# Feed-forward up products taken on x times the norm weight, with the root of the norm applied behind them

## The chip, the core and the metric

The kernel runs on one core of a Trainium2 chip. The metric is the device time of one execution in microseconds (us), as the median of several runs. The kernel works in float32 kept as two halves: each operand is split into a rounded part ("h") and a rest ("l"), and each product is the sum of three passes of TensorE, h·h, h·l and l·h. TensorE (PE) multiplies, VectorE (DVE) makes the rests and the sums, ScalarE (ACT) makes the rounded parts and the activations, GpSimd (POOL) starts accumulating transfers, and SyncE (SP) starts the loads.

## What is computed

One macaron block: a feed-forward (FFN), a mixer, a second FFN and a last norm, on 512 tokens of width 1024; the hidden width of an FFN is 2816, or 22 tiles of 128 columns. Cut to what matters here:

```python
def rmsnorm(x, g):
    y = x * lax.rsqrt(jnp.mean(x * x, axis=-1, keepdims=True) + EPS)
    return y * g

def swiglu(x, w_gu, w_down):
    g, u = jnp.split(x @ w_gu, 2, axis=-1)
    return (jax.nn.silu(g) * u) @ w_down

x = x + 0.5 * swiglu(rmsnorm(x, g1), ffn1_w_gu, ffn1_w_down)
x = x + hybrid_mixer(rmsnorm(x, gm), w_in, ...)
x = x + 0.5 * swiglu(rmsnorm(x, g2), ffn2_w_gu, ffn2_w_down)
return rmsnorm(x, gf)
```

The root, 1/sqrt(mean(x²) + eps), is one number for each token. It can be put on x before the product, or on the product's rows after it.

## The kernel before

Activations lie transposed: `x[k]` is the k-th 128 of the 1024 columns, by 512 tokens. An FFN's up half makes 22 hidden tiles, each from a gate column block and an up column block of 128.

**Three kinds of products.** A *plain* tile multiplies weights (stationary) with x (moving, 512 tokens): 2 column blocks, 8 depths and 3 passes, 48 passes of 512 columns each. A *tall set* makes four tiles by seven products in place of eight, from sums of blocks of the weights and of the activations; it has 14 steps (7 products in two halves) of 12 passes of 512 columns, 168 passes, with the activations stationary and the weights moving. A *set* makes two tiles by the same seven products in 168 passes of 256 columns. The products are named m1, p2, q6, p5, q7, p3 and p4; m1, q6, q7 and p4 add up in one PSUM bank, and what is in it has to be copied out by ACT before the next of them is added. A tall set's result has tokens on the partitions, so it is turned by `turn`: 16 transposes of 128x128 on PE.

**Order before.** Each FFN takes the first four hidden tiles as plain tiles, on x times the norm weight (no root), and multiplies the results with the root, `row`, laid out along the tokens (`plain_pair`). FFN 1 then has four tall sets and a set, FFN 2 a tall set, a set and three tall sets. Those work on the fully normed x: `normed` writes x·g·row into eight free tiles of `hid` (L757), and `Operands.make` splits its blocks and block sums (L676, L677). The class `Norm` splits x·g as each x[k] comes (L499, L500) and adds the squares (L505, L508, L509); `rstd_rows` sums them with two products against ones (L529, L530), transposes, takes the root and spreads it.

**What sets the order.** A scheduler places the instructions of each engine; each engine runs its queue in that order, and within the sets the order of PE is written by hand. Weights come as tiles of 512 KB named `f` (ten buffers) on SP's queue (L358). `Weights.issue` casts each to `wh` on ACT (L393) and makes the rest `wl` on DVE (L394), two steps ahead of the product. The sums of weight blocks are made in place: by transfers that add `f` to `f`, started on POOL (L362), and by subtractions on DVE (L372 for a tall set, and L387 for a set's extra sum). The mixer between the FFNs starts with loads of two small arrays, `wgl` and `gup` (L1140, L1153), into its buffers `tp`; the products of `wgl` are L1165 and L1166. It ends with the output products of `w_o`, of which eight tiles x[0] to x[7] are finished one after the other on DVE (L1624).

Of the kernel before, what the change touches and what calls it, by code (L numbers as in the profile page):

```python
# [8 lines left out]
F32 = mybir.dt.float32  # L9
# [94 lines left out]
PLAIN1, PLAIN2 = 4, 4  # L104
# [27 lines left out]
TALL_ORDER = ("m1", "p2", "q6", "p5", "q7", "p3", "p4")  # L132
TALL = {}


def tall(name, mat, cols, base=0):
# [6 lines left out]
    STEPS.extend((n, p) for p in TALL_ORDER for n in firsts)  # L143

# [13 lines left out]
def up_plan(up, plain, slow):  # L158

    kinds = ["tall"] * ((KF - plain) // 4)  # L160
    kinds.insert(len(kinds) if slow else 1, "set")
    f = plain
    for kind in kinds:
        if kind == "tall":
            tall((up, f), up, (f * P, DFF + f * P))
# [8 lines left out]
UPS = {}  # L174


def ffn_plan(up, down, plain, slow):
# [38 lines left out]
ffn_plan("ffn1_w_gu", "ffn1_w_down", PLAIN1, True)  # L216
mixer_plan()
ffn_plan("ffn2_w_gu", "ffn2_w_down", PLAIN2, False)
# [8 lines left out]
def block_kernel(ctx: ExitStack, tc: tile.TileContext, xT, vecs, gf, gup, wgl, wts, out):  # L227
# [79 lines left out]
    class Weights:  # L307
# [15 lines left out]
        def phase(self, early, first=6):  # L323
# [4 lines left out]
            for i in range(lo, self.end):  # L328
                n, p = STEPS[i]
                if p == "m1" and n in TALL:  # L330
                    self.loads.setdefault(i - (4, 3)[TALL[n][1]], []).append(n)
                    self.firsts.setdefault(i - (1, 0)[TALL[n][1]], []).append(n)
# [31 lines left out]
        def issue(self):  # L364
            at = self.issued
            self.fetch(at)
            for n in self.loads.get(at, ()):
                self.raw[n] = [self.dma(n + i) for i in range(4)]
# [144 lines left out]

    def rstd_rows(accs, width):
# [47 lines left out]
    class Set:  # L562
# [8 lines left out]

        def run(self, p):
            b = {"m1": "b", "p2": "a", "q6": "b", "p5": "c", "q7": "b", "p4": "b", "p3": "c"}[p]
            if self.group.joint:
                return self.run_joint(p, b)
# [6 lines left out]
            for k in range(4):  # L582
                for e in range(2):
                    s = slice(k * HW + e * P, k * HW + (e + 1) * P)
                    t = slice(k * HW, (k + 1) * HW)
                    to = o[:, e * HW : (e + 1) * HW]
                    for j, (ww, aa) in enumerate(((h, bh), (h, bl), (l, bh))):
# [9 lines left out]
        def run_joint(self, p, b):  # L597
            fresh = b not in self.bank
            two_banks = b != "b"
            if fresh:  # L600
                self.bank[b] = MM2() if two_banks else MM()
            o = self.bank[b]
            parts = self.group.get(p)
            h, l = W.take()
            for k in range(4):
                a = parts[k // 2][:, (k % 2) * S : (k % 2 + 1) * S]
                for e in range(2):
                    s = slice(k * HW + e * P, k * HW + (e + 1) * P)
                    if two_banks:
                        nc.tensor.matmul(o[:, e], h[:, s], a, start=fresh and k == 0,  # L610
                                         stop=False, skip_group_check=True)
                        nc.tensor.matmul(o[:, e, HW:], l[:, s], a[:, :HW], start=False,
                                         stop=k == 3, skip_group_check=True)
                        continue
                    to = o[:, e * HW : (e + 1) * HW]
                    for j, (ww, aa) in enumerate(((h, a[:, :HW]), (h, a[:, HW:]),
                                                  (l, a[:, :HW]))):
                        nc.tensor.matmul(to, ww[:, s], aa, start=fresh and k == 0 and e == 0 and j == 0,
                                         stop=k == 3 and j == 2, skip_group_check=True)
            if p in self.keep:  # L620
                v = T()
                nc.scalar.copy(v, o)
                self.v[p] = v
            self.done(self, p)

    class Operands:
# [5 lines left out]
        def __init__(self, b, joint=False):  # L632
            self.b = b
            self.joint = joint
            self.parts = {}
            self.sums = set()
# [20 lines left out]
        def make(self, p):  # L657
            if p in self.parts:
                return
            i = self.ORDER.index(p)  # L660
            if i > 0:
                self.make(self.ORDER[i - 1])
            v = self.sum(p)
            if self.joint:
                t = [tile_of("op", [P, 1024], F32R) for _ in range(2)]
                for i in range(2):
                    a = t[i].rearrange("p (k b t) -> p k b t", b=2, t=HW)
                    vi = v[:, 2 * i : 2 * i + 2]
                    nc.scalar.copy(a[:, :, 0], vi)
                    nc.vector.tensor_tensor(out=a[:, :, 1], in0=vi,  # L670
                                            in1=a[:, :, 0].bitcast(F32), op=ALU.subtract)
                self.parts[p] = t
                return
# [61 lines left out]
    def ffn(up, down, norm, nxt, plain, at):  # L735
        xh, xl = norm.h, norm.l
        rows = []

        def finish(k):
            if k == at:  # L740
                rows.append(norm.finish())
# [35 lines left out]
        for f in range(2, plain):  # L777
            g = mm_single(up, KD, f * P, xh, xl)
            u = mm_single(up, KD, DFF + f * P, xh, xl)
            if f == 2:  # L780
                xo.make("p5")
# [916 lines left out]
```

## Time and profile before

| | |
|---|---|
| Median of 3 runs | 1174.08 us (1173.42 to 1174.63) |
| The profiled execution | 1173.56 us, of which its span is 1171.8 us |
| PE busy | 1161.5 us, 99% of the span |
| DVE busy | 899.6 us, 77% |
| ACT busy | 643.0 us, 55% |
| Up half of FFN 1, from the first product on x to the first down product | 5.7 to about 230 us |
| Mixer | about 343 to 829 us |
| Up half of FFN 2 | about 829 to 1064 us |

A row of the timeline reads: start, duration, engine, line, operation, output and inputs with the buffer numbers left out, shape, count; in square brackets how long the engine had been idle and what ended it. "PEclk" is the granted share of the TensorE clock.

### The profile page before, as it was taken

The numbers are of one execution on the slowest core, as the hardware profiler recorded it, in microseconds if no ns is written. First come the engines' busy times: TensorE is split into PE (matmuls) and PEld (weight loads), VectorE is DVE, ScalarE is ACT, GpSimd is POOL, SyncE is SP. The second block draws the span as 40 slices with busy tenths as digits, with TensorE's granted clock in tenths as the row PEclk, the third lists the DMA queues.
The fourth block names the chain that finished last, engine by engine and source line by source line (L and its number), as shares of the span: only waits on it lengthen the run. The fifth ranks groups of instructions, "written<-read, shape, count | busy, mean of one in ns | idle before, by whom it ended". The sixth has DMA issues, their size and how long they took to land.

```text
span 1171.8 us, 16449 instructions
## 1 busy us (share of the span) xinstructions
PE 1161.5 (99%) x6410; PEld 1012.3 (86%) x6410; DVE 899.6 (77%) x1081; ACT 643.0 (55%) x811; POOL 121.6 (10%) x161
## 2 busy tenths in 40 slices
PE   9999999999999999999999999999999999999997
PEld 8888888999988888789999998888888988888886
DVE  7985657879887976777797999556598566699965
ACT  6555555635452757474654577524356555575543
POOL 0101110011110110111010112000010111101100
PEclk9999999999999999999999999999999999999999
DMA  9667785647485485877566788811746777867711
GB/s 362 132 187 170 173 221 154 170 121 180 104 283 144 93 219 155 201 206 208 141 162 158 176 201 220 288 36 50 247 112 158 195 191 155 205 177 171 179 49 72
DMA packets 59006, 200.07 MB, mean 171 GB/s; under 512 B 6865, under 2 KB 6993, under 8 KB 58929
## 3 DMA queue, kind: packets, MB, share of 16 engines
q0 software_dynamic: 19424, 70.26, 31.7%
q1 hardware_dynamic: 36912, 124.27, 31.5%
q10 hardware_dynamic: 2592, 4.49, 1.0%
q8 instruction: 50, 0.82, 0.3%
q14 instruction: 28, 0.22, 0.1%
HBM read 124.55 MB, written 8.39 MB: 113 GB/s over the span
## 4 chain that ended last, share of the span: by engine, by line
PE 96%; DVE 2%; ACT 1%; issue 1%; DMA 0%; POOL 0%; DVEq 0%; ACTq 0%; POOLq 0%
PE mm L704 44%; PE mm L588 22%; PE mm L445 7%; PE mm L422 3%; PE mm L423 3%; PE mm L421 3%; PE mm L464 1%; PE mm L463 1%; PE mm L462 1%; PE aux L826 1%; PE mm L1020 1%; PE mm L1018 1%; PE mm L1019 1%; DVE wl L394 1%; PE aux L1320 1%
## 5 line engine op out<-in xcount | busy, mean ns | idle before, releaser
L393 ACT CAST wh<-f 128x1024 fp32r<-128x1024 f32 (+1 forms) x343 | 359.2, 1048 | 381.2 <-PE mm L704 120.3
L394 DVE TENSOR_TENSOR wl<-f,wh 128x1024 fp32r<-128x1024 f32 (+1 forms) x343 | 416.8, 1218 | 184.9 <-ACT wh L393 180.1
L704 PE MATMUL mm<-wh,op 128*128 128x512 f32 x1568 | 492.4, 391 | 0.0
L704 PEld LDWEIGHTS mm<-wh,op 128*128 128x128 f32 x1568 | 294.4, 188 | 60.4
L704 PE MATMUL mm<-wl,op 128*128 128x512 f32 x784 | 305.7, 390 | 0.7 <-DVE wl L394 0.7
L588 PE MATMUL mm<-op,wh 128*128 128x256 f32 x1568 | 284.6, 284 | 0.6 <-ACT tp L593 0.6
L588 PEld LDWEIGHTS mm<-op,wh 128*128 128x128 f32 x1568 | 245.0, 192 | 1.7 <-ACT tp L593 0.8
L588 PE MATMUL mm<-op,wl 128*128 128x256 f32 x784 | 222.2, 283 | 1.1 <-DVE wl L394 1.1
L362 POOL DMA_DIRECT2D f<-f x126 | 108.6, 863 | 919.4 <-DVE wl L394 336.4
L704 PEld LDWEIGHTS mm<-wl,op 128*128 128x128 f32 x784 | 147.3, 188 | 31.2 <-DVE wl L394 1.5
L588 PEld LDWEIGHTS mm<-op,wl 128*128 128x128 f32 x784 | 150.3, 192 | 1.6 <-DVE wl L394 1.5
L445 PE MATMUL mm<-op,wh 128*128 128x512 f32 x256 | 64.0, 391 | 0.0
L421 PE MATMUL mm<-op,wh 128*128 128x512 f32 x164 | 63.8, 389 | 0.0
L422 PE MATMUL mm<-op,wh 128*128 128x512 f32 x164 | 63.8, 389 | 0.0
L423 PE MATMUL mm<-op,wl 128*128 128x512 f32 x164 | 63.8, 389 | 0.0
L445 PEld LDWEIGHTS mm<-op,wh 128*128 128x128 f32 x256 | 48.0, 188 | 10.3 <-issue 0.2
L676 ACT CAST op<-hid 128x1024 fp32r<-128x1024 f32 x42 | 43.9, 1048 | 18.7 <-PE mm L704 12.7
L677 DVE TENSOR_TENSOR op<-hid,op 128x1024 fp32r<-128x1024 f32 x42 | 51.2, 1220 | 3.6 <-ACT op L676 3.4
L387 DVE TENSOR_TENSOR f<-f,f 128x1024 f32<-128x1024 f32 x28 | 34.2, 1221 | 5.6 <-DMA f<-f 4.6
L421 PEld LDWEIGHTS mm<-op,wh 128*128 128x128 f32 x164 | 30.8, 188 | 6.5
L422 PEld LDWEIGHTS mm<-op,wh 128*128 128x128 f32 x164 | 30.8, 188 | 6.4
L423 PEld LDWEIGHTS mm<-op,wl 128*128 128x128 f32 x164 | 30.8, 188 | 6.3
(283 smaller groups left out, 1146.0 us busy)
## 6 DMA issues: line engine op xcount, KB each, us to landing
f<-wts SPq DMA_DIRECT2D x219, 512.0 KB, 4.3
f<-f POOLq DMA_DIRECT2D x126, 512.0 KB, 5.0
X<-xT SPq DMA_DIRECT2D x8, 256.0 KB, 5.3
xs<-X POOLq DMA_DIRECT2D x8, 256.0 KB, 6.3
ga<-tp ACTq DMA_DIRECT2D x8, 256.0 KB, 4.9
gb<-tp ACTq DMA_DIRECT2D x8, 256.0 KB, 3.8
tp<-ga SPq DMA_DIRECT2D x8, 256.0 KB, 4.8
X<-xs POOLq DMA_DIRECT2D x8, 256.0 KB, 7.4
```

The lines of the kernel that those rows point to most:

```text
L362: nc.gpsimd.dma_start(out_, a, accum_op=ALU.add)
L387: nc.vector.tensor_tensor(out=a11, in0=a11, in1=a22, op=ALU.subtract)
L393: nc.scalar.copy(h[:, :w], raw[:, :w])
L394: nc.vector.tensor_tensor(out=l[:, :w], in0=raw[:, :w], in1=h[:, :w].bitcast(F32), op=ALU.subtract)
L421: nc.tensor.matmul(o, wh, ah, start=first, stop=False)
L422: nc.tensor.matmul(o, wh, al, start=False, stop=False)
L423: nc.tensor.matmul(o, wl, ah, start=False, stop=last)
L445: nc.tensor.matmul(o[c], w[:, s : s + P], a[k], start=k == 0 and j == 0, stop=k == kt - 1 and j == 2)
L588: nc.tensor.matmul(to, ww[:, s], aa[:, t], start=fresh and k == 0 and e == 0 and j == 0, stop=k == 3 and j == 2, skip_group_check=True)
L676: nc.scalar.copy(hv, v)
L677: nc.vector.tensor_tensor(out=lv, in0=v, in1=hv.bitcast(F32), op=ALU.subtract)
L704: nc.tensor.matmul(self.bank[b][e], aa[:, c], ww, start=fresh and i == 0 and n == 0, stop=k == 3 and n == 2, skip_group_check=True)
```

## The change

The new class `Gain` takes the place of `Norm` for the two FFNs. The up products are taken on x·g, and the root is applied to their results: as the scale of the Silu and in the multiplication behind it. In tall sets the tokens lie on the partitions, so the root is a column of 128 numbers per token block: `finish` sums the squares by four products of one column each (L569) and takes the root on 128x4 numbers; nothing is transposed or spread.

In FFN 1 the first two hidden tiles stay plain, but with activations stationary and the four weight blocks moving (`GU`), and their results are turned on PE (`turn_pair`, 8 transposes); the other 20 are five tall sets. In FFN 2 nothing is plain: a tall set, a set, and four tall sets, the set with activations stationary (`Turned`) and turned by `turn_pair`. For the tall sets x·g is written whole into the free tiles of `hid` by eight ACT instructions (L773). In FFN 1 `Gain` besides splits it as x comes, in blocks of 256 tokens, which serve as operands of the plain tiles and of the products m1, p2 and p3. The order of the products differs by set: the first tall set of FFN 1 takes p5 ahead of q6, the first and last of FFN 2 take p5 ahead of p2. The first down products of FFN 1 leave two of the eight banks for the end, so that the last tall set can be turned in between, and the buffers `tp` of the mixer move behind its others.

```diff
-PLAIN1, PLAIN2 = 4, 4
+FIRST1 = ("m1", "p2", "p5", "q6", "q7", "p3", "p4")
+FIRST2 = ("m1", "p5", "p2", "q6", "q7", "p3", "p4")
...
-def up_plan(up, plain, slow):
+def up_plan(up, first):
-    kinds = ["tall"] * ((KF - plain) // 4)
-    kinds.insert(len(kinds) if slow else 1, "set")
+    kinds = ["tall"] * ((KF - first) // 4)
+    if first == 0:
+        kinds.insert(1, "set")
...
-    units(group(up, KD, (0, DFF, P, DFF + P), slow))
-    for f in range(2, plain):
-        units(single(up, KD, f * P))
-        units(single(up, KD, DFF + f * P))
-    up_plan(up, plain, slow)
+    if slow:
+        units(group(up, KD, GU, True))
+    up_plan(up, 2 if slow else 0)
...
+    class Gain:
...
+                for l in ls:
+                    h, w = (t[:, i * HW : (i + 1) * HW] for t in self.parts[j, l])
+                    v = x[k][:, l * HW : (l + 1) * HW]
+                    if sooner and k == 0:
+                        nc.vector.tensor_scalar(out=h, in0=v, scalar1=g, scalar2=None,
+                                                op0=ALU.mult)
+                    else:
+                        nc.scalar.activation(h, v, AF.Copy, scale=g)
+                    nc.vector.scalar_tensor_tensor(out=w, in0=v, scalar=g, in1=h.bitcast(F32),
+                                                   op0=ALU.mult, op1=ALU.subtract)
...
+        def finish(self):
+            st = AUX()
+            for t in range(NTB):
+                nc.tensor.matmul(st[:, t : t + 1], self.acc[:, t * P : (t + 1) * P],
+                                 ones[:, 0:1], start=True, stop=True)
...
+            newton_rsqrt(r, v, s, q)
...
+    class Turned(Set):
+        def products(self, bh, bl, h, l):
+            return (bh, h), (bh, l), (bl, h)
...
-    def ffn(up, down, norm, nxt, plain, at):
...
+    def ffn(up, down, hid, norm, nxt):
+        XN = KF - KD
+        for k in range(KD):
+            nc.scalar.activation(hid[:, XN + k], x[k], AF.Copy, scale=norm.g(k))
...
+            norm.finish()
+            plain.extend(T() for _ in range(2))
+            for t in range(NTB):
+                v = plain[t // 2][:, (t % 2) * HW : (t % 2 + 1) * HW]
+                nc.scalar.activation(v, o[t][:, :HW], AF.Silu, scale=norm.r[t])
+                nc.vector.scalar_tensor_tensor(out=v, in0=o[t][:, HW:], scalar=norm.r[t], in1=v,
+                                               op0=ALU.mult, op1=ALU.mult)
...
-                        nc.scalar.activation(g[t], g[t], AF.Silu)
+                        nc.scalar.activation(g[t], g[t], AF.Silu, scale=norm.r[t])
...
-                        nc.vector.scalar_tensor_tensor(out=g[t], in0=b, scalar=-1.0, in1=g[t],
-                                                       op0=ALU.mult, op1=ALU.mult)
+                        nc.vector.scalar_tensor_tensor(out=g[t], in0=b, scalar=norm.minus[t],
+                                                       in1=g[t], op0=ALU.mult, op1=ALU.mult)
...
-    with phase("small2", f=10, tp=6, v=4, qk=2, g=1, y=1, small=1):
+    with phase("small2", f=10, v=4, qk=2, g=1, y=1, small=1, tp=6):
```

Three places where instructions move are shown here, in the order in which the engines run them.

ACT near the start of FFN 1, before: the last gain and the last square of x, then the casts of the next weights (`wh`) and the first half of the split of the sum of squares.

```order
L499 ACTIVATE op_178<-X,vec 128x512
L508 ACTIVATE tp_187<-X 128x512
L393 CAST wh_216<-f_206 128x1024
L393 CAST wh_234<-f_208 128x1024
L472 CAST tp_302<-acc_143 128x512
L393 CAST wh_270<-f_210 128x1024
L393 CAST wh_322<-f_212 128x1024
```

The same place now; `wh_251` is the cast for depths 4 and 5 of the plain tiles, the counterpart of `wh_216`.

```order
L555 ACTIVATE op_175<-X,vec 128x256
L555 ACTIVATE op_177<-X,vec 128x256
L562 ACTIVATE tp_204<-X 128x512
L773 ACTIVATE hid_119<-X,vec 128x512 x7
L408 CAST wh_251<-f_231 128x1024
L408 CAST wh_268<-f_233 128x1024
L408 CAST wh_296<-f_235 128x1024
```

Each gain has become two of half the width, and seven of the eight gains into `hid` stand between the last square and the cast.

DVE at the start of FFN 2, before: from the finishing of x[7] on, through rests of plain weights, the sum of squares and the root.

```order
L1624 TENSOR_TENSOR X_7004<-mm_7609,X_7004 128x512
L394 TENSOR_TENSOR wl_7691<-f_7668,wh_7690 128x1024
L500 SCALAR_TENSOR_TENSOR op_7636<-X_7004,vec,op_7635 128x512
L509 TENSOR_TENSOR acc_7486<-acc_7486,tp_7645 128x512
L473 TENSOR_TENSOR tp_7789<-acc_7486,tp_7788 128x512
L394 TENSOR_TENSOR wl_7721<-f_7670,wh_7720 128x1024
L394 TENSOR_TENSOR wl_7757<-f_7672,wh_7756 128x1024
L394 TENSOR_TENSOR wl_7809<-f_7682,wh_7808 128x1024
```

The same place now: rests of tall weights (L409), operand sums (L693, L696, L698) and their rests (L712).

```order
L1683 TENSOR_TENSOR X_6940<-mm_7527,X_6940 128x512
L409 TENSOR_TENSOR wl_7627<-f_7602,wh_7626 128x1024
L563 TENSOR_TENSOR acc_7422<-acc_7422,tp_7557 128x512
L693 SCALAR_TENSOR_TENSOR hid_7576<-hid_7576 128x4x256
L712 TENSOR_TENSOR op_7663<-hid_7576,op_7662 128x1024
L409 TENSOR_TENSOR wl_7643<-f_7604,wh_7642 128x1024
L712 TENSOR_TENSOR op_7722<-hid_7576,op_7721 128x1024
L409 TENSOR_TENSOR wl_7669<-f_7610,wh_7668 128x1024
L696 TENSOR_TENSOR hid_7576<-hid_7576 128x4x256
L409 TENSOR_TENSOR wl_7686<-f_7612,wh_7685 128x1024
L698 SCALAR_TENSOR_TENSOR hid_7576<-hid_7576 128x4x256
```

The run goes on in the same way to the second in-place subtraction of weight blocks, `f_7600` (L402), 25 instructions behind that of x[7]: 15 of 128x1024, 3 of 128x512 and 7 of 128x4. On ACT the cast that reads this `f_7600` (`wh_7797`) is followed at once by the two copies of product q6's banks (L826).

SP ahead of the mixer, before: `wgl` and `gup` are loaded ahead of the mixer's weights.

```order
L358 DMA f_3006<-wts 128x1024
L1140 DMA tp_3244<-wgl 128x128
L1153 DMA tp_3256<-gup 16x512 x6
L358 DMA f_3205<-wts 128x1024
L358 DMA f_3207<-wts 128x1024
```

The same place now, from the last of those weight tiles on.

```order
L367 DMA f_3288<-wts 128x1024
L367 DMA f_3290<-wts 128x1024
L367 DMA f_3292<-wts 128x1024
L1199 DMA tp_3180<-wgl 128x128
L1212 DMA tp_3192<-gup 16x512 x6
L367 DMA f_3399<-wts 128x1024
```

Twelve weight tiles, `f_3141` to `f_3292`, now stand ahead of the two small arrays.

More of the change, by code (lines that the diff above doesn't have):

```diff
@@ L595, in run, with products, __init__ @@
             self.done(self, p)
[L597 to L624, printed above, removed]
+    class Turned(Set):
+        def products(self, bh, bl, h, l):
+            return (bh, h), (bh, l), (bl, h)
     class Operands:
         ORDER = ("m1", "p2", "p5", "q6", "q7", "p3", "p4")
-        def __init__(self, b, joint=False):
+        def __init__(self, b, order_=ORDER, parts=()):
             self.b = b
-            self.joint = joint
-            self.parts = {}
+            self.order = order_
+            self.parts = dict(parts)
             self.sums = set()
@@ L838, in done @@
                     nc.vector.tensor_tensor(out=s.g1, in0=bank["a"], in1=v["m1"], op=ALU.add)
-                    nc.scalar.activation(s.g1, s.g1, AF.Silu)
+                    for t in range(2):
+                        c = slice(t * HW, (t + 1) * HW)
+                        nc.scalar.activation(s.g1[:, c], s.g1[:, c], AF.Silu, scale=norm.r[t])
                 if p == "q7":
@@ L1637, in block_kernel @@
         W.phase(1)
-        n1 = Norm(V_G1)
+        n1 = Gain(V_G1, blocks=True)
+        hid = tile_of("hid", [P, KF, S])
         for k in range(KD):
```

223 lines of the change are left out of this document (134 added, 89 removed).

## The prediction

> **What bounds the kernel now.** The page comes first, then what PE waited for, then the chain of work that ended last.
>
> ```profile
> span 1171.8 us, 16449 instructions
> PE 1161.5 (99%) x6410; PEld 1012.3 (86%) x6410; DVE 899.6 (77%) x1081; ACT 643.0 (55%) x811; POOL 121.6 (10%) x161
> PE 96%; DVE 2%; ACT 1%; issue 1%; DMA 0%; POOL 0%; DVEq 0%; ACTq 0%; POOLq 0%
> ```
>
> PE works 99% of the span. The view of waits has four rows for it, 3.5 us in all, and none lies in an FFN's up half:
>
> ```profile
> PE mm L588 <- DVE wl L394: 1.1, 2, 0.6
> PE aux L292 <- POOL ones L289: 1.1, 1, 1.1
> PE mm L704 <- DVE wl L394: 0.7, 1, 0.7
> PE mm L588 <- ACT tp L593: 0.6, 1, 0.6
> ```
>
> So the FFNs run at PE's own pace. A pass that is taken away is worth its pace; a wait that is put in costs its whole length, since nothing else is slack. The paces stand in long pieces of the chain (start, length, what, count):
>
> ```profile
> 50.11 43.52 PE mm L704 x192
> 93.63 0.87 PE aux L826 x8
> 251.48 80.63 PE mm L588 x672
> ```
>
> A pass of 512 columns takes 43.52/192 = 0.2267 us, one of 256 columns 80.63/672 = 0.1200 us (0.0066 more than half), a transpose 0.87/8 = 0.109 us. The other engines have little room where operands are made:
>
> ```profile
> 0.00:28.20 28.20, 27.09 (x119) 23.00 (x120) 21.45 (x36) 19.11 (x28) 2.13 (x10) 1.00 0.95 363
> 851.00:873.00 22.00, 22.00 (x99) 18.21 (x98) 21.11 (x33) 9.91 (x12) 2.38 (x3) 1.00 0.44 106
> ```
>
> (After the span come PE, weight loads, DVE, ACT and POOL.) In the first 28.2 us ACT is busy 19.1 us; before FFN 2's first tall set DVE is busy 21.1 of 22 us, and that is under plain tiles, whose unit of weights lasts 24 passes. A tall unit lasts 12.
>
> **PE's work.** The counts come from the code. The first plain tiles of FFN 1 have 96 passes before and now; I take that stretch below, as a whole. The rest of FFN 1's up half had 96 plain passes, four tall sets (672) and a set (168 half passes); now it has five tall sets, 840. That is 72 × 0.2267 = +16.3, −168 × 0.1200 = −20.2, and 24 transposes more (16 for the fifth tall set, 8 for the plain pair), +2.6: **−1.3 us**. FFN 2's up half had 192 plain passes, 2 of the norm, 672 tall and 168 half passes; now it has 840 and the same 168, so −26 × 0.2267 = −5.9, again 24 transposes, +2.6, and four one-column products for the root. No row has a product of one column; below it is bounded by nothing, above by two 128-column pieces each, 8 × 0.109 = 0.9, and I take 0.4. Together **−2.9 us**. PE saves 4.2 us.
>
> **The start of FFN 1.** This is the largest term. The rows of the timeline, first the whole start, then the casts:
>
> ```profile
> 5.68 2.22 PE L445 MATMUL mm<-op,wh 128*128 128x512 f32 x8
> 6.63 0.62 ACT L393 CAST wh<-f 128x512 fp32r<-128x512 f32 x1
> 13.88 0.70 ACT L499 ACTIVATE op<-X,vec 128x512 fp32r<-128x512 f32 x1
> 14.49 0.62 ACT L508 ACTIVATE tp<-X 128x512 f32<-128x512 f32 x1
> 15.01 1.98 ACT L393 CAST wh<-f 128x1024 fp32r<-128x1024 f32 x2
> 16.83 3.49 DVE L394 TENSOR_TENSOR wl<-f,wh 128x1024 fp32r<-128x1024 f32 x3
> 17.48 1.05 ACT L393 CAST wh<-f 128x1024 fp32r<-128x1024 f32 x1
> 28.18 0.39 PE L421 MATMUL mm<-op,wh 128*128 128x512 f32 x1
> ```
>
> ACT's queue is packed: a gain of 512 columns moves it on by 14.49 − 13.88 = 0.61 us. Before, the cast for depths 4 and 5 starts at 15.01, and the stretch ends at 28.18. Now ACT has more ahead of this cast. Eight gains into `hid`: 8 × 0.61 = 4.9. And 14 gains of 256 columns for 7 of 512. No row has ACT gaining 256 columns: bounded by 0.61 (no cheaper) and 0.31 (exactly half). The casts say which: 1.05 us for 1024 columns and 0.62 for 512, so 256 columns fewer save 0.215, which gives 0.40. So 14 × 0.40 − 7 × 0.61 = +1.3. The cast starts at 15.01 + 6.2 = 21.2 and ends at 22.3. On DVE an operand sum of 1024 columns (L696) that reads the last gain stands ahead of the cast's rest; each moves DVE on by (3.49 − 1.22)/2 = 1.135, the last 1.22 being the row's single duration. The rest is there at 21.3 + 1.135 + 1.22 = 23.7. Three of the 48 passes of depths 4 to 7 need no rest; 45 × 0.2267 = 10.2 remain, so the stretch ends near 34.0 in place of 28.18, **+5.8 us**. The half-width price moves this from +4.5 to +8.7. PE is done with depths 0 to 3 well ahead: it begins at 5.7 plus some 0.5, since DVE now makes the first gain in halves, and 48 × 0.2267 = 10.9 more is 17.1. The sum of squares is whole near 18 (ACT's last square ends where its last seven gains begin, at 21.2 − 7 × 0.61 = 16.9, and DVE adds it). So PE waits about 1 us, runs the four one-column products, and waits about 4 us for the cast and 1 for its rest. Behind it, the first weight sums have cover: the first tall set's p5 starts 11 us after the stretch.
>
> **The start of FFN 2.** The last w_o pass ends at T. Two products that need only depths 0 to 3 (m1, p5), then p2, then q6, are 96 passes; with the root's columns PE is ready for q7 at T + 21.8 + 0.4 = T + 22.2. But q7 goes into q6's bank, which ACT copies behind the cast `wh_7797`, and this waits for DVE's subtraction `f_7600`.
>
> ```profile
> 828.72 0.69 DVE L1624 TENSOR_TENSOR X<-mm,X 128x512 f32<-128x512 f32 x1 [2.05 <-PE mm L423]
> 28.91 1.28 DVE L559 TENSOR_TENSOR tp<-mm,row 128x512 f32<-128x512 f32 x2
> 847.15 0.18 DVE L533 TENSOR_SCALAR st_v<-tp 128x16 f32<-128x16 f32 x1
> L796 ACT COPY tp<-mm x16: 587/589/592, 54.9 to 1019.8; 128x512 f32<-128x512 f32 x16
> ```
>
> DVE finishes x[7] near T + 0.8. Up to the subtraction stand 15 instructions of 1024 columns (15 × 1.135 = 17.0), 3 of 512 (1.28 for two gives 0.60 each: 1.8) and 7 tiny ones (0.18 each: 1.3): 20.1 us, so T + 20.9. Then the cast, 1.05, and two copies, the first of which moves ACT on by about 0.5 and the second takes 0.59: T + 23.0. PE waits 0.8 us. This holds if the weights are there. The first rest of that run reads `f_7602`, which POOL's transfer makes from two loads in a queue of eight:
>
> ```profile
> 817.76 18.21 SPq L358 DMA_DIRECT2D f<-wts  x11
> DMA to landing us min/median/max: 3.5/6.8/9.5
> f<-f POOLq DMA_DIRECT2D x126, 512.0 KB, 5.0
> DMA to landing us min/median/max: 4.6/5.7/6.8
> ```
>
> (The second row is of the nine loads issued from 817.76 to 825.4; the last of POOL's two additions between 26 and 34 us, of which the slower, 6.8 us, was started among loads as they are here.) The loads of FFN 2 were issued about 11 us before x[7] was finished. The third of such a queue lands some 5 us after its issue, between the least, 3.5, and the middle, 6.8, and the addition 5.0 to 6.8 later: near T. From 0 to 2 us of delay come on top; the term is 0 to 2.8 and I take **+1.2 us**.
>
> **Small waits.** `wgl` is now issued behind twelve loads instead of ahead of them.
>
> ```profile
> 312.50 0.33 SPq L1140 DMA_DIRECT2D tp<-wgl  x1
> DMA to landing us min/median/max: 3.3/3.3/3.3
> 348.56 0.33 SPq L358 DMA_DIRECT2D f<-wts  x1
> 343.02 11.11 PE mm L445 x49
> 354.13 0.23 PE aux L1165
> ```
>
> It was issued 41 us before its product and took 3.3 us to land. Now it follows the twelfth load, which before was issued 5.5 us into the mixer (348.56 − 343.02). Its product stands 59 passes into the mixer now, 49 before: 59 × 0.2267 = 13.4 us. So some 8 us remain for landing, a rest of weights on DVE and the split of `wgl`: from 0 to 1.5 is lost, and I take **+0.3**. The same copy of a bank ahead of the next product, three times elsewhere (FFN 1's first tall set, the down product behind the last `turn`, FFN 2's last tall set), is worth 0 to 0.3 each: **+0.5**.
>
> **The sum.** +5.8 − 1.3 − 2.9 + 1.2 + 0.3 + 0.5 = +3.6 us on the profiled execution's 1173.56, which is 1177.2. That execution lies 0.5 under the median of the runs, so against 1174.08 I predict **1177.7 us**, 0.31% slower. Other edits cost nothing that ends on the path: the root in the Silu's scale is the same instruction on ACT, the removed transposes and spread of the row were under plain passes.
>
> [...] The trace at its end shows when the clock falls (start:end, PE busy, and PEclk as the third number from the right):
>
> ```profile
> 1165.00:1168.00 3.00, 0.01 (x1) 0.00 (x0) 2.55 (x8) 1.33 (x4) 0.00 (x0) 1.00 0.46 174
> 1169.00:1170.00 1.00, 0.00 (x0) 0.00 (x0) 0.00 (x0) 0.00 (x0) 0.00 (x0) 0.97 0.97 367
> 1170.00:1171.80 1.80, 0.00 (x0) 0.00 (x0) 0.00 (x0) 0.00 (x0) 0.00 (x0) 0.50 0.22 88
> ```
>
> PE ended at 1165.0 and had the full clock until past 1169: about 4.9 us of idleness. The start's longest wait in one piece is shorter, about 4 us, so the sum has no loss of clock.
>
> [...]
>
> **Rivals.**
>
> *Half-width work at half price, nothing else late: not slower.* If ACT's fixed part counts little, the 14 gains cost 0.31 each and the start is +4.5; with FFN 2's weights landing early (0.4) and no small waits, −4.2 + 4.5 + 0.4 = +0.7, 1174.8. For it: the ranges allow it. Against: the casts' slope, and the packed DVE queue of FFN 2. The point: with the other waits at these lower ends the whole stays under 2.3 us for a start under 6.1, a half-width price of 0.42; with them as I take them, only from 0.31 down. Chance 0.20. A stronger form, in which the gains into `hid` cost no time because ACT takes them in gaps, gives −4.2 + 0.5 + 1.2 = −2.5, 1171.6; against it stands that the queue has them behind the last square, with no gap. Chance 0.05.
>
> *The clock falls in the start's wait.* The first products of the program show half pace:
>
> ```profile
> 1.11 4.64 PE L292 MATMUL aux<-ones 128*128 128x128 f32 x20 [1.11 <-POOL ones L289]
> ```
>
> That is 0.232 us for a piece of 128 columns which takes 0.109 later. Such a stretch of 4.6 us would lose 2.3: 1180.0. Chance 0.10.
>
> *Transfers late.* Loads and additions of FFN 2 and `wgl` at their upper ends: 2.8 and 1.5 for 1.2 and 0.3, so +2.8, 1180.5. For it: POOL's 6.8 us under load. Against: 5.0 us is usual. Chance 0.15.
>
> *It does not do what it says* in one point: SP's first eleven rows, x among the first weights, are the same before and now. That part moves nothing, and the sum has nothing for it.
>
> **Chances.** The forecast holds 0.50. A measurement of this kernel tells 0.2%, 2.3 us, from no change: slower means over 1176.4. The forecast, the clock and the transfers are slower, but for a little of the forecast: 0.73. The mild form of the first rival is no change: with that little, 0.22. The stronger one is faster: 0.05. The range goes from 1174.9, the first rival, to 1181.8, the transfers and half of what the clock would add.
>
> **What would show it.** After the change: PE idle for 4 to 6 us in all between 17 and 24 us, ended by ACT's cast and then DVE's rest; the next stretch (the first tall set) beginning near 34; PE waiting about 1 us for L826's copies some 22 us behind w_o; PE's passes at the same paces. It is wrong if the first wait is under 3 us, if PEclk shows a dip in the first slice, or if a wait over 1 us stands in a tall set after the first.

## The result, and the profile after

The changed kernel takes 1185.0 us (median; 1182.8 to 1185.5), the kernel before 1173.9 on the same chip. The ratio is 1.009, with a 95% interval from 1.0073 to 1.0108: slower by three times what was forecast (1177.7), and above the range.

The page of the changed kernel shows more work on PE, not less:

```profile
span 1183.7 us, 16373 instructions
PE 1166.0 (99%) x6350; PEld 1009.7 (85%) x6350; DVE 888.1 (75%) x1050; ACT 668.6 (56%) x855; POOL 129.9 (11%) x170
```

The page counts 60 instructions of PE fewer than before, and 4.5 us more of busy time. The work was to shrink by 4.2 us, so some passes must have been slower. What PE waited for:

```profile
PE mm L739 <- ACT tp L826: 2.6, 1, 2.6
PE mm L794 <- ACT wh L408: 2.5, 1, 2.5
PE mm L739 <- DVE wl L409: 1.7, 2, 1.1
...
PE aux L1224 <- DVE g L1209: 0.3, 1, 0.3
```

(After the colon: us in all, times, the longest.) Two waits of 2.5 us stand out, one at the start of FFN 1 (L794, the plain group) and one at the start of FFN 2 (L739, ahead of q7).

Where the time went, by stage: each stage begins with the row of PE's timeline that starts it, in one profiled execution of each kernel (1185.4 us for the changed one).

| us | before | after | difference | forecast |
|---|---|---|---|---|
| Start, to the end of the first plain tiles | 28.18 | 35.58 | +7.40 | +5.8 |
| Rest of FFN 1 | 314.68 | 314.21 | −0.47 | −1.0 |
| Mixer | 485.66 | 486.66 | +1.00 | +0.3 |
| FFN 2, first product to last `turn` | 234.80 | 238.75 | +3.95 | −1.5 |
| Rest | 108.48 | 108.50 | 0.0 | 0 |

(Of the prediction's 0.5 for small waits, 0.3 is counted in FFN 1 and 0.2 in FFN 2.) The differences add up to 11.9, that of the two spans. Two thirds of the miss are in FFN 2, a fifth at the start.

**The start.** PE's rows at the end of depths 0 to 3, and the first row of the first tall set:

```profile
18.15 1.05 PE L569 MATMUL aux<-ones,acc 128*128 128x1 f32 x8 [0.30 <-DVE acc L563]
21.71 1.65 PE L794 MATMUL mm<-wh,op 128*128 128x512 f32 x3 [2.50 <-ACT wh L408]
23.17 0.79 PE L795 MATMUL mm<-wl,op 128*128 128x512 f32 x1
...
35.58 0.39 PE L739 MATMUL mm<-wh,op 128*128 128x512 f32 x1
```

The cast and its rest come at 21.7 and 23.2, half a microsecond sooner than forecast. From there the 45 passes that remain should have taken 10.2 us, to 33.4. They took 12.4. Of the signs of being wrong that the prediction named, two are here: the wait for the cast, 2.50, is under 3 us, and PEclk falls in the first slice. ACT's queue shows why the cast is there only at 21.7, and that the half-width price was right (two gains in 0.80 us, from 13.70 to 14.50):

```profile
13.70 0.90 ACT L555 ACTIVATE op<-X,vec 128x256 fp32r<-128x256 f32 x2
14.50 0.62 ACT L562 ACTIVATE tp<-X 128x512 f32<-128x512 f32 x1
...
16.34 4.38 ACT L773 ACTIVATE hid<-X,vec 128x512 f32<-128x512 f32 x7
20.63 2.92 ACT L408 CAST wh<-f 128x1024 fp32r<-128x1024 f32 x3
```

**The clock.** Windows at both places (start:end, length, PE busy and its passes, PEclk, DMA share, GB/s):

```profile
20.00:21.00 1.00, 0.00 (x0) 0.93 1.03 410
21.00:22.00 1.00, 0.29 (x1) 0.50 1.01 406
...
24.00:25.00 1.00, 1.00 (x3) 0.50 0.57 152
...
27.00:28.00 1.00, 1.00 (x4) 0.66 0.81 238
...
862.00:863.00 1.00, 0.00 (x0) 1.00 0.00 0
863.00:864.00 1.00, 0.69 (x3) 0.97 0.00 0
...
866.00:867.00 1.00, 1.00 (x4) 0.50 1.28 197
867.00:868.00 1.00, 1.00 (x6) 0.82 0.67 188
```

The clock is halved from about 20.9 to 27.7 and again from 863.94 to 867.4; passes then stand 0.43 us apart in place of 0.23. At the start 4.5 of the half-speed microseconds lie behind the rest's arrival and cost 2.2; in FFN 2 it is 3.4 us, worth 1.7. In FFN 2 the clock fell when PE was already back at work: the charge came behind the wait.

**FFN 2.** DVE's timeline, with the two subtractions for q7 (L402, one for each half of the product):

```profile
839.27 1.23 DVE L409 TENSOR_TENSOR wl<-f,wh 128x1024 fp32r<-128x1024 f32 x1 [1.93 <-ACT wh L408]
...
847.83 1.22 DVE L409 TENSOR_TENSOR wl<-f,wh 128x1024 fp32r<-128x1024 f32 x1
...
855.43 1.23 DVE L402 TENSOR_TENSOR f<-f,f 128x1024 f32<-128x1024 f32 x1 [2.79 <-DMA f<-f]
856.65 1.22 DVE L409 TENSOR_TENSOR wl<-f,wh 128x1024 fp32r<-128x1024 f32 x1
...
860.40 1.22 DVE L402 TENSOR_TENSOR f<-f,f 128x1024 f32<-128x1024 f32 x1
```

POOL's timeline, with the transfers that it started before them, and then the time to landing of the six that it started from 828.8 to 849.3:

```profile
847.07 0.85 POOL L371 DMA_DIRECT2D f<-f  x1 [5.12 <-DVE wl L409]
849.35 0.86 POOL L371 DMA_DIRECT2D f<-f  x1 [1.42 <-DVE wl L409]
```

```profile
DMA to landing us min/median/max: 4.5/8.1/10.5
```

DVE stands still twice. The first time it is 1.93 us, ahead of the first rest: the cast that makes its operand waited for the first addition, which was started at 828.76 and took 9.3 us to land. The second time it is 2.8 us, ahead of the first subtraction. This one overwrites the weight block a11, and the transfer started at 847.07 reads a11 to add it into a12. It landed 8.3 us later. The rest at 856.65, which q6's second half needs, stands behind the subtraction (PE's wait of 1.1), and so does the second subtraction, then ACT's cast, then the copies of the bank (ACT's timeline, and behind it PE's):

```profile
861.73 1.04 ACT L408 CAST wh<-f 128x1024 fp32r<-128x1024 f32 x1 [1.08 <-DVE f L402]
862.68 0.58 ACT L826 COPY tp<-mm 128x512 f32<-128x512 f32 x1
```

```profile
863.31 0.50 PE L739 MATMUL mm<-wh,op 128*128 128x512 f32 x1 [2.60 <-ACT tp L826]
```

### The profile page after: what moved, and what is told of

Read it like the earlier page. It is cut to its first block, busy times and chain, and to the rows that moved or that the text cites. A ratio compares the mean times of both kernels' runs of the same rounds, so it can differ in the third digit from the quotient of the medians.

```text
span 1183.7 us, 16373 instructions
## 1 busy us (share of the span) xinstructions
PE 1166.0 (99%) x6350; PEld 1009.7 (85%) x6350; DVE 888.1 (75%) x1050; ACT 668.6 (56%) x855; POOL 129.9 (11%) x170
## 5 line engine op out<-in xcount | busy, mean ns | idle before, releaser
L409 DVE TENSOR_TENSOR wl<-f,wh 128x1024 fp32r<-128x1024 f32 (+1 forms) x352 | 427.8, 1218 | 200.1 <-ACT wh L408 199.7
L739 PE MATMUL mm<-wh,op 128*128 128x512 f32 x1792 | 565.1, 392 | 2.6 <-ACT tp L826 2.6
L739 PEld LDWEIGHTS mm<-wh,op 128*128 128x128 f32 x1792 | 337.2, 188 | 73.2 <-ACT tp L826 3.9
L739 PE MATMUL mm<-wl,op 128*128 128x512 f32 x896 | 349.9, 391 | 1.7 <-DVE wl L409 1.7
L657 PE MATMUL mm<-op,wh 128*128 128x256 f32 x1344 | 243.7, 284 | 0.1
L657 PEld LDWEIGHTS mm<-op,wh 128*128 128x128 f32 x1344 | 209.9, 192 | 0.9 <-ACT tp L662 0.3
L739 PEld LDWEIGHTS mm<-wl,op 128*128 128x128 f32 x896 | 168.8, 188 | 36.9 <-DVE wl L409 3.0
L657 PE MATMUL mm<-op,wl 128*128 128x256 f32 x672 | 190.5, 284 | 1.1 <-DVE wl L409 1.1
L657 PEld LDWEIGHTS mm<-op,wl 128*128 128x128 f32 x672 | 128.9, 192 | 1.6 <-DVE wl L409 1.5
L712 DVE TENSOR_TENSOR op<-hid,op 128x1024 fp32r<-128x1024 f32 x39 | 47.4, 1219 | 3.5 <-ACT op L711 3.4
L402 DVE TENSOR_TENSOR f<-f,f 128x1024 f32<-128x1024 f32 x32 | 39.1, 1222 | 12.0 <-DMA f<-f 10.4
L436 PE MATMUL mm<-op,wh 128*128 128x512 f32 x100 | 39.1, 391 | 0.0
L438 PE MATMUL mm<-op,wl 128*128 128x512 f32 x100 | 38.9, 389 | 0.0
L437 PE MATMUL mm<-op,wh 128*128 128x512 f32 x100 | 38.9, 389 | 0.0
L460 PE MATMUL mm<-op,wh 128*128 128x512 f32 x128 | 31.9, 391 | 0.0
L460 PEld LDWEIGHTS mm<-op,wh 128*128 128x128 f32 x128 | 23.9, 188 | 5.0
L478 PE MATMUL mm<-wl,op 128*128 128x512 f32 x64 | 25.0, 391 | 0.2 <-DVE wl L409 0.2
L477 PE MATMUL mm<-wh,op 128*128 128x512 f32 x64 | 25.1, 392 | 0.0
```

Source lines behind the costliest of these rows:

```text
L402: nc.vector.tensor_tensor(out=a11, in0=a11, in1=a22, op=ALU.subtract)
L409: nc.vector.tensor_tensor(out=l[:, :w], in0=raw[:, :w], in1=h[:, :w].bitcast(F32), op=ALU.subtract)
L436: nc.tensor.matmul(o, wh, ah, start=first, stop=False)
L437: nc.tensor.matmul(o, wh, al, start=False, stop=False)
L438: nc.tensor.matmul(o, wl, ah, start=False, stop=last)
L460: nc.tensor.matmul(o[c], w[:, s : s + P], a[k], start=k == 0 and j == 0, stop=k == kt - 1 and j == 2)
```

## Experiments

Times are medians; "won" is against the changed kernel's 1185.0. The kernel before, run beside each of them, took 1173.5 to 1174.3.

**Gains behind the casts (e1).** In `ffn`:

```diff
-        for k in range(KD):
-            nc.scalar.activation(hid[:, XN + k], x[k], AF.Copy, scale=norm.g(k))
+        def gains():
+            for k in range(KD):
+                nc.scalar.activation(hid[:, XN + k], x[k], AF.Copy, scale=norm.g(k))
+        if nxt is None:
+            gains()
...
+            gains()
             norm.finish()
```

> In FFN 1 the eight gains into hid are issued behind the products of the plain group, so that the casts of depths 4 to 7 stand ahead of seven of them on ACT. Theory (ACT's queue sets the start, and the clock falls only because PE stands idle): the cast for depths 4 and 5 ends near 17.5 in place of 21.7, PE waits 1.0 us or less for it and its rest, PEclk stays at 1.00, and the first tall set begins at 30.0 to 30.5 in place of 35.58: 5.3 us less than the changed kernel, 1179.7. If the clock falls all the same (one-column products do not count as work), 2.2 of that is not won: 1181.9. Rival (a load of weights or a rest on DVE stands right behind the cast): the wait only changes its name, 1 to 2 us are won, 1183.5.

Measured: 1177.95 us (1175.8 to 1180.3), 1.0037 of the kernel before (1.0024 to 1.0050); 7.0 won. In the profiled execution (1175.8, the fastest of five) the first tall set begins at 29.93, as expected, and the waits are:

```profile
PE mm L739 <- ACT tp L831: 2.3, 1, 2.3
PE mm L798 <- DVE op L552: 1.2, 1, 1.2
...
PE mm L798 <- ACT wh L408: 0.2, 1, 0.2
```

So the gains into `hid` ahead of the cast are what the start waits for, and nothing stands right behind it: 5.65 us of the start's 7.40, with the clock's part in it. More was won than that, because FFN 2, where nothing was edited, took 235.54 us in place of 238.75. It still waits 2.3 us for the copies (DVE stands 2.13 and 0.95 us), but this time the clock does not fall:

```profile
853.00:855.00 2.00, 0.00 (x0) 1.00 0.00 0
855.00:856.00 1.00, 0.72 (x3) 1.00 0.00 0
856.00:859.00 3.00, 3.00 (x15) 1.00 1.02 177
```

So a wait of this size may or may not cost a half-speed stretch; what the traces show of the difference stands behind the next two runs. The other executions of this kernel spread over 2.6 us, and their mean granted clock is 0.997 to 0.998 for this one's 0.999, which would fit, though only the profiled one shows where.

**Kept awake (e3, e8).** The changed kernel with passes whose results nobody reads:

```diff
+    FIRST_TALL = []
...
+    def warm_up(a):
+        o = AUX()
+        for _ in range(10):
+            nc.tensor.matmul(o, a[:, :P], a[:, :512], start=True, stop=True)
...
+                if u[1] == 4:
+                    warm_up(parts[0, 0][0])
                 h, l = W.take(u)
...
+            if p == "q7" and s == 0 and FIRST_TALL and self is FIRST_TALL[-1]:
+                warm_up(self.group.get("m1")[0])
...
+            FIRST_TALL.append(talls[up, UPS[up][0][1]])
```

> The changed kernel with ten passes of 512 columns, whose results nobody reads, put into each of PE's two long waits (ahead of depths 4 of FFN 1, and ahead of q7 of FFN 2's first tall set); 10 x 0.2267 = 2.3 us each, within waits of 2.5 and 2.6. Theory (the clock falls because PE does nothing for some 3 us): PEclk stays at 1.00 in both places, the passes behind keep the pace of 0.2267, and the kernel is 2.2 + 1.7 = 3.9 us faster for doing more, 1181.1. Rival (the passes behind the waits are slow for another reason, such as the transfers under way): the same time or up to 1 us more, 1185 to 1186.

Measured: 1181.87 us (1180.5 to 1183.2); 3.1 won for 4.5 us of useless work. In FFN 2 it went as expected: the idle passes fill the wait and PEclk is 1.00 throughout:

```profile
859.34 2.43 PE L723 MATMUL aux<-op 128*128 128x512 f32 x10
862.10 0.50 PE L748 MATMUL mm<-wh,op 128*128 128x512 f32 x1 [0.32 <-ACT tp L837]
```

The up half took 235.80 in place of 238.75. At the start it did not: behind the one-column products and a last wait of 1.2 us the clock fell after all, from 21.9 to 25.3, and the first tall set began at 34.15. With 14 passes in place of 10:

> The run that kept PE awake, with 14 idle passes ahead of depths 4 of FFN 1 in place of 10, so that they last until the cast is there. In that run PEclk still fell in FFN 1, from 21.93 to 25.1, behind the one-column products and a wait of 1.2 us. Theory (one-column products count as idle, and a stretch of 3.4 us that is idle by half or more halves the clock for the next one): PE now stands idle for 1 us at most, PEclk stays at 1.00, and the first tall set begins at 33.2 to 33.7 in place of 34.15 (35.58 in the changed kernel); the time is 0.5 us less than in that run. Rival (the clock falls for another reason at this place): PEclk shows 0.50 again, and the first tall set begins at 35 or later.

Measured: 1180.26 us (1179.8 to 1182.5); 4.7 won. Now the start keeps its clock:

```profile
20.00:23.00 3.00, 2.50 (x15) 1.00 1.04 411
23.00:26.00 3.00, 2.16 (x9) 1.00 0.36 131
26.00:29.00 3.00, 3.00 (x15) 1.00 1.01 295
```

The first tall set begins at 33.96, though, and not at 33.2 to 33.7, because the rest came at 23.84, 0.7 us later than in e3: the one-column products now ended a microsecond later, and in DVE's queue the instruction that reads them (L573, at 21.35 in place of 20.34) stands ahead of the operand sum and the rest. In the changed kernel the clock fell at both places, behind waits of 2.50 and 2.60 us; with passes put into the waits PEclk stays at 1.00 in FFN 2 (e3, e8) and at the start (e8).

The traces also show how much work PE had ahead of a fall. In the changed kernel's record of the clock the changes lie 6.827, 836.265, 3.413 and 314.026 us apart: 2, 245, 1 and 92 times 3.4133. In that of the kernel before the only two changes lie 1163.945 us apart, 341 times as much. Marks 3.41 us apart, laid from a change of the run itself, divide PE's work into stretches:

| run, stretch with full clock | full passes, us | one-column products, us | the clock behind it |
|---|---|---|---|
| changed kernel, 860.53 to 863.94 | 0.81 | 0 | fell |
| e4, 853.64 to 857.05 | 1.21 | 0 | fell |
| e3, 18.44 to 21.86 | 1.25 | 0.95 | fell |
| e2, 860.06 to 863.48 | 1.41 | 0 | fell |
| e8, 19.88 to 23.29 | 1.67 | 0.95 | stayed |
| e5, 1171.51 to 1174.93 | 1.76 | 0 | stayed |
| e1, 850.78 to 854.19 | 2.20 | 0 | stayed |
| e1, 854.19 to 857.61 | 2.33 | 0 | stayed |

In these rows the clock fell behind the stretches with up to 1.41 us of full passes and stayed behind those with 1.67 or more. That a stretch must be "idle by half or more" was the author's estimate from the runs before it: by its letter e8's own, with 1.67 of 3.41, should have cost the clock too. The wait of 2.3 us in e1 lies across a mark, that of 2.6 us in the changed kernel between two. One-column products did not keep the clock up in e3 as passes did in e1: with them, e3's stretch would have 2.20 us of work, as much as e1's first, behind which the clock stayed.

**What FFN 2 waits for (e2, e5).** First, another order of products in its first tall set:

```diff
-                o = FIRST1 if first else FIRST2
+                o = FIRST1 if f == first else FIRST2
...
-            xo = Operands(gained, FIRST2)
+            xo = Operands(gained, FIRST1)
...
-            at_step(((up, UPS[up][0][1]), 1, "p5"), norm.finish)
+            at_step(((up, UPS[up][0][1]), 0, "p2"), norm.finish)
```

> In FFN 2 the first tall set takes its products in FFN 1's order, p2 ahead of p5, and the one-column products move between the two halves of p2; so the transfer that adds a11 into a12 is issued one product, 5.4 us, sooner. Theory (the subtraction of q7 waits until that transfer has read a11): PE's wait of 2.6 us ahead of q7 falls to 1.3 or less, the 1.1 us ahead of q6 goes, and with the wait goes the stretch at half clock (1.7): 3.5 to 5 us less than the changed kernel, near 1181. Rival (the length of DVE's own queue sets it, as the prediction had it): the wait stays within 0.8 us of 2.6, or goes to p2's operand, and at most 1.5 us are won, 1183.5 or more.

Measured: 1183.34 us (1181.5 to 1184.5); 1.7 won. By its time this is the rival: the waits ahead of q7 are 1.45 and 1.26, together no shorter, and the clock falls again. But DVE still stands idle, now ahead of the second subtraction:

```profile
854.13 1.23 DVE L402 TENSOR_TENSOR f<-f,f 128x1024 f32<-128x1024 f32 x1
857.88 1.23 DVE L402 TENSOR_TENSOR f<-f,f 128x1024 f32<-128x1024 f32 x1 [2.53 <-issue]
```

The transfers follow one another (POOL's waits there are for `f<-f`), so that an earlier start of the product moved the last of them only from 849.35 to 846.71. This last one took 11.1 us to land, to 857.8, and the second subtraction begins right then, at 857.88. So the time is the rival's, but the trace points to the transfer, though it names no releaser for this wait. The next run takes the dependence away:

```diff
-                    s3 = a11
+                    s3 = a21
                     if p == "q7":
-                        nc.vector.tensor_tensor(out=a11, in0=a11, in1=a22, op=ALU.subtract)
+                        nc.vector.tensor_tensor(out=a21, in0=a11, in1=a22, op=ALU.subtract)
```

> The changed kernel, but the subtraction for q7 writes a11 - a22 into a21, which p5 is done with, and no longer over a11; so it need not wait until the transfer that adds a11 into a12 has read a11. Theory (FFN 2's wait is that transfer, not DVE's work): DVE's idle time of 2.8 us ahead of the subtraction goes, PE's waits of 2.6 and 1.1 us in FFN 2's first tall set fall to 1 in all, PEclk stays at 1.00 there, and the stretch from the first pass of FFN 2's up half to its last transpose falls from 238.75 to about 234: 4 to 5 us less than the changed kernel, 1180 to 1181. Rival (DVE has too much to do, as the prediction's sum had it): the wait becomes a wait for another row of DVE, at most 1.5 us are won, 1183.5 or more.

Measured: 1180.98 us (1180.4 to 1181.8), 1.0061 of the kernel before (1.0047 to 1.0074); 4.0 won. FFN 2's up half takes 233.93, and in it PE waits once:

```profile
PE mm L739 <- ACT tp L826: 0.5, 1, 0.5
```

That wait stands at 1046.26, in the last tall set; in the first one no wait is left. The subtractions are done earlier (at 849.08 and 852.68), DVE has no gap around them, and PEclk is 1.00 there. The first of them runs while the transfer that reads a11, started at 847.19 and 4.8 us to landing, is still under way. So FFN 2's waits hung above all on that transfer, and not on the amount of DVE's work. A smaller part is not the edit's: PE reaches FFN 2 1.2 us later in this execution, its first addition lands no later than in the changed kernel, and DVE stands only 0.84 us ahead of its first rest in place of 1.93.

**Both (e4).** The edits of e1 and e2 together.

> The later gains of FFN 1 and FFN 1's order in FFN 2 together. Theory: the two waits are apart, so the gains add, 5.3 + 4.3 = 9.6 us less than the changed kernel, 1175.4; what remains above the kernel before is the start's 2 us (half-width gains, one-column products), about 1 in FFN 2, 1 in the mixer and 0.8 in FFN 1's tall sets, against 4.2 saved on PE. Rival (something else bounds both): less than 7 us won, above 1178.

Measured: 1178.49 us (1177.0 to 1179.2); 6.5 won, the rival's answer, since e2's edit mends little. In its profiled execution FFN 2's up half takes 237.34, with the clock down again. The start is 1.2 us longer than in e1, with nothing edited there and no wait longer than e1's: the first products run at half pace,

```profile
8.61 0.63 PE L800 MATMUL mm<-wh,op 128*128 128x512 f32 x1
9.04 0.63 PE L798 MATMUL mm<-wh,op 128*128 128x512 f32 x1
9.46 0.63 PE L799 MATMUL mm<-wl,op 128*128 128x512 f32 x1
...
10.66 0.39 PE L799 MATMUL mm<-wl,op 128*128 128x512 f32 x1
```

0.43 us apart until 10.3. From 6 to 10 us this execution has 9 passes, that of the changed kernel 15.

**The mixer's buffers in their old place (e9).**

```diff
-    with phase("small2", f=10, v=4, qk=2, g=1, y=1, small=1, tp=6):
+    with phase("small2", f=10, tp=6, v=4, qk=2, g=1, y=1, small=1):
```

> The changed kernel with the mixer's buffers tp back in their old place, second in line behind the weights. The prediction had this part of the change as a cost alone (wgl later, +0.3). Theory (by what has been seen of FFN 2's loads since: a buffer of the next stage is free only when what lay at its place is): FFN 2's weights then share their place with buffers that the mixer's last products hold, the wait for them comes ahead of FFN 2's first tall set, and the kernel gets slower by several us, up to 10. Rival (the prediction): the 0.3 us at wgl's product goes, nothing else moves, 1184.5 to 1185.

Measured: 1192.75 us (1192.7 to 1192.8); 7.8 lost. The size is the theory's, the place is not. POOL's first transfers of FFN 2 start at 828.86, as in the changed kernel (828.76); what is late is `hid`, which now lies over `tp`:

```profile
841.17 5.00 ACT L773 ACTIVATE hid<-X,vec 128x512 f32<-128x512 f32 x8 [1.36 <-DVE acc L563]
```

All eight gains come in one piece behind the last square of x, and PE waits 9.6 us for the first operand. The move of `tp` is no mere cost of 0.3: without it the first tall set of FFN 2 waits 9.6 us.

**All mended (e6, e10, e7).** In e6, besides e1's and e5's edits, the squares of depths 4 to 7 move behind the casts, PE begins with the tokens that DVE splits first, and `hid` comes ahead of the weights in FFN 2:

```diff
+            if self.parts is None or k < 4:
+                self.square(k)
...
+                if u[1] == 4:
+                    for k in range(4, KD):
+                        norm.square(k)
+                    norm.finish()
+                    gains()
...
-                    for t in range(NTB):
+                    for t in (2, 3, 0, 1) if k < 4 else range(NTB):
...
-    with phase("small3", **FFN):
+    with phase("small3", hid=1, f=10, tp=9):
```

> What the runs so far point to, in one kernel: the subtraction as in the run before; FFN 1's gains into hid and the squares of depths 4 to 7 behind the casts of the plain group's weights; PE's first products on the half of the tokens that DVE splits first; and hid ahead of the weights in FFN 2's buffers, so that its loads need not wait for the last weights of w_o. Theory: the first tall set begins near 29 in place of 35.58, FFN 2's up half is near 233 in place of 238.75 and the clock never falls, 6.6 + 5.7 = 12.3 less than the changed kernel: about 1172.5, 1171 to 1173.5, as fast as the kernel before or up to 0.2% faster. Rival (the work on ACT and DVE that was moved stands in the way later, in the first tall set): 1175 or more.

Measured: 1174.63 us (median of 11 executions), 1.0009 of the kernel before (1.0000 to 1.0018): 10.4 won of the 12.3 expected, and not faster than before. The start (28.92) is as expected and FFN 2's up half (234.36) 1.4 above. Another 1.3 are lost late in the mixer, at a product of `w_out_gla` that the edits don't touch, where a cast on ACT stands behind an instruction that waits for a transfer:

```profile
736.94 0.63 ACT L1649 ACTIVATE tp<-tp 128x512 f32<-128x512 f32 x1 [4.71 <-DMA tp<-ga]
737.48 1.03 ACT L408 CAST wh<-f 128x1024 fp32r<-128x1024 f32 x1
```

The same waits (0.4 to 0.6 and 0.8) stand in the profiled executions of e3 and e5, the second of them in e10's below, and neither in e1's.

> The run with everything mended, but with hid back behind the weights in FFN 2's buffers. Theory (once the subtraction does not wait for the transfer, when the loads come matters little): FFN 2's up half is 234 to 235 us, within 0.7 of that run, and the time is 1173.5 to 1175. Rival (the earlier loads were what mended FFN 2): a wait of 1 us or more is back there, 1176 or more.

Measured: 1174.41 us (median of 12), 1.0003 (0.9995 to 1.0012). The start takes 28.54, FFN 2's up half 233.91. The earlier loads were not needed.

> The kernel before with the same change of the subtraction. Theory: its tall sets all have a plain tile or another set in front, so no transfer is late there, and the time stays within 0.5 us of the kernel before. Rival (the subtraction costs PE time in every tall set): 2 us or more faster.

Measured: 1174.19 us (median of 10), 1.0001 (0.9992 to 1.0010): as expected, e5's edit mends what the change made, and does nothing for the kernel before.

So with both waits gone the change is worth nothing that can be measured. By stage, e10 against before: start +0.4, rest of FFN 1 −0.4, mixer +1.3, FFN 2 −0.9.

## Why the prediction was wrong

The direction was right, and so was the mechanism of the largest term; the size failed, by 8.2 us in the profiled execution.

*"The start of FFN 1", +5.8.* The gains into `hid` ahead of the cast, the half-width price of 0.40, the wait and its two causes were as forecast; e1 confirms that they are the cause. Up to the rest's arrival the stretch went by the sum, 0.5 better. What failed is the sentence "so the sum has no loss of clock". It took the longest wait, 4 us, against the 4.9 of idleness at the trace's end. But the trace's end is one example, not a threshold; by the marks of 3.41 us, its 4.9 us are the end of a stretch that still held 1.9 us of passes, and a whole one with none (1166.53 to 1169.94). The start's wait was 2.5 us long and the clock fell. The rival *The clock falls in the start's wait*, given 0.10, came true, and it came true a second time in FFN 2, where the prediction did not look for it. That its price agrees, 2.3 for a measured 2.2, is luck: the 2.3 came from a half-speed stretch of 4.6 us at the program's beginning, and of the 6.8 us measured here 4.5 happened to lie behind the rest.

In the changed kernel the half-speed stretch in FFN 2 lasts 3.41 us and the one at the start 6.83, twice that, while e1's wait of 2.3 us went free. The stretches ahead of a fall were not idle as a whole: the 3.41 us that ended at 863.94 held 0.8 us of passes, and e2's held 1.4. The fall at the start came again in e3, e5 and e9 (PEclk 0.88 from 12 to 24 us and 0.83 from 24 to 36 in the last two), so the chance given to this rival was too small.

*"The start of FFN 2", +1.2.* This is the term that failed most: the waits are 3.7, and with the clock (1.7) and the one-column products (0.8 for 0.4) the stage is at +3.95 where −1.5 was forecast. The sum of DVE's chain, 20.1 us, was not the limit; the 4.7 us that DVE stood idle in it were. Of these, 1.93 are the first addition, for which the sum had 0 to 2 us and took little. The other 2.79 are the step that is missing, the transfer that reads a11: the prediction followed the first addition, which makes `f_7602`, and stopped there, although the subtraction "f_7600" needs the third one to have landed. Its bound of 5.0 to 6.8 us for an addition was too low as well; these six had a median of 8.1. The rival *Transfers late* was right that the additions come late, and for the first of them nearly right in how much; it had neither the wait for a transfer that still reads what is to be overwritten, nor the clock behind it.

*PE's work, −4.2.* The counts of passes hold, but less of them arrives. FFN 1's rest gained 0.47 for 1.0. In FFN 2 a stage with only 0.5 us of waits (e5) is 0.9 below the kernel before, where 2.9 were counted; the one-column products take 0.4 of that and the wait 0.5. The remaining 1.1 was not settled; part of it may be that PE's rows stand 0.08 us further apart at each change between passes and transposes (0.31 us for 0.23 from 81.10 to 81.41, behind eight transposes), of which there are more now.

*"wgl later", +0.3.* Measured 0.3 at that place (L1224). The mixer's other 0.7 stay open: its other listed waits are 0.5 more than before (L1360, L478) and 0.6 less (the wait for `tp` ahead of L588). *Small waits, +0.5:* at 58.02 in FFN 1 and at 1048.82 in FFN 2 two passes take 0.88 us in place of 0.61, which is 0.27 at each of these places. *"x loaded first" moves nothing:* the start gives no sign otherwise.

## What to carry to other kernels

Where PE is busy 99% of the span, an edit that saves passes must leave a head start in front of every stage that it shortens: a stage that begins with its hardest operands shows every dependence that plain work used to hide. Follow each operand of the new first stage back to the transfers, including those that only *read* what will be overwritten; writing to a place that is already free (e5) may mend it for nothing. And price a wait on PE like those seen here (2.50 and 2.60 us in the changed kernel, 1.45 and 1.26 close together in e2) with the half-speed stretch that may come behind it: 6.83 and 3.41 us in the changed kernel, none behind e1's 2.3.

## What the runs showed that was not expected

- Behind a wait of 2.6 us the clock was halved for 3.4 us, although PE was at work again when it fell; behind a wait of 2.3 us at the same place, which lay across a mark of the 3.41 us, it was not (e1). It fell behind 0.95 us of one-column products and a wait of 1.2 us (e3), and stayed behind as much of them and waits of 0.3 and 1.05 (e8).
- PEclk does not show the slow beginning: in e4 the products are 0.43 us apart until 10.3 us, and the window says 1.00. The trace's record of the clock begins only with a change at 10.55, so the 1.00 ahead of it is no measurement:

```profile
6.00:10.00 4.00, 3.66 (x9) 1.00 1.03 385
10.00:14.00 4.00, 4.00 (x18) 1.00 1.05 414
```

- Ten to fourteen passes of useless work in a wait made the kernel faster (e3 by 3.1 us, e8 by 4.7).
- Four products of one column take 0.8 to 1.05 us, as much as four passes of 512 columns (0.91).
- The order in which buffers are laid out was worth 7.8 us (e9), without one instruction more or less.
